# Seven half products for eight: the feed-forward column pairs of a two-layer hybrid network on one core

## Chip, core and metric

The kernel runs on one core of one Trainium2 chip. The metric is device time in microseconds of one execution. The kernel before takes 2122.2 us, the median of three runs (2119.26 to 2122.68).

## What is computed

Two layers over 512 tokens of width 1024, all in fp32. Each layer has a feed-forward block, a mixer (in layer 0 latent attention and a gated delta rule, in layer 1 sparse attention), a second feed-forward block and a gated embedding (PLE). The change touches the four feed-forward blocks:

```python
def swiglu(h, w_gu, w_down):          # w_gu: 1024 x 5632, w_down: 2816 x 1024
    g, u = jnp.split(h @ w_gu, 2, axis=-1)
    return (jax.nn.silu(g) * u) @ w_down

for i in range(DEPTH):
    x = x + 0.5 * swiglu(rms_norm(x, ln_ffn1[i]), ffn1_w_gu[i], ffn1_w_down[i])
    ...                               # x = x + mixer(rms_norm(x, ln_mix[i]))
    x = x + 0.5 * swiglu(rms_norm(x, ln_ffn2[i]), ffn2_w_gu[i], ffn2_w_down[i])
    ...                               # x = x + sigmoid(rms_norm(x, ln_ple[i]) @ w_gate) * (p[i] @ w_in)
```

## The kernel before

The activations lie transposed: x is eight tiles of 128 features by 512 tokens. `prep` multiplies each by its norm gain and splits it into a high part (fp32r) and a low part (the rest); the row factor of the norm, `rB`, is applied to results instead. `mm3` makes one fp32 product from three fp32r matmuls: high by high, high by low, low by high. Each is a 128x128 weight tile against 512 token columns.

`ffn` goes over 22 column pairs j. A pair is column block j of the gate half of `w_gu` and block j of the up half, 128 columns each. For each, `proj` calls `weights`, which loads 1024x128 weights in one DMA of 512 KB on SP into a `raw` tile, casts the high part on ACT and subtracts the low part on DVE (`split`, whose subtraction may also go to POOL as `flex`). It then runs eight k-steps of `mm3` into one PSUM bank. The gate is multiplied by rB (DVE), goes through Silu (ACT) and is multiplied by rB again (POOL); the up result times that is the activation, split again into two big tiles that stay until the down projection. After all 22 pairs the down projection goes over eight output blocks d, each with 22 k-steps in three weight loads; the result is added to x[d] by DVE and `prep(d)` follows for the next stage.

Inside the mixers `weights` splits another way (`split_dma`): ACT writes the high part and minus the weights, and POOL issues a DMA that adds the raw weights to the latter.

The order of instructions on every engine is written out ahead by `Order.issue`. Each operation has a price (`price`, line 335 on); the list scheduler keeps a clock for each engine, takes the ready operation with the smallest key (its place in TensorE's program order, less a part of its longest way to the end), and fixes the order. Tiles come from pools with limits: 58 big tiles of 2 KB a partition (`c`), 4 raw and 3 + 3 split weight tiles of 4 KB, 8 temporaries, 8 PSUM banks. Every tile operation is emitted at one line, L313, so groups in the profile are told apart by tile names: `raw_t`, `wh_t` and `wl_t` are weights, `c_t` big tiles, `t_t` temporaries, `p_t` PSUM banks, `x` the residual.

The start loads x, and the first weights of the first pair between the x tiles (`first`, `early`).

Of the kernel before, what the change touches and what calls it, by code (L numbers as in the profile page):

```python
# [17 lines left out]
P = 128  # L18
# [65 lines left out]
class Op:  # L84
    __slots__ = ("eng", "fn", "cost", "preds", "succs", "tiles", "left", "ready", "done", "forms", "key", "ahead")


KAPPA = 0.9
PEN, TAU, THR = 30.0, 5.0, 0.8
# [3 lines left out]
class Order:  # L93
# [78 lines left out]
    def issue(self):  # L172
# [57 lines left out]
        while len(order) < n:  # L230
# [21 lines left out]
            for e in engines:  # L252
                while idle[e] <= now and avail[e]:
                    i = heapq.heappop(avail[e])[1]
                    tag = fits(i)
                    if tag is not None:
                        blocked[tag].append(i)
                        continue
                    op = ops[i]
                    order.append(i)  # L260
                    issued[i] = True
                    while first < n and issued[first]:
                        first += 1
                    if op.fn[0] == "dma_start":
                        idle[e] = now + (0.45 if e == "sync" else 0.9)
                        dma = max(dma, now + (1.3 if e == "sync" else 2.6)) + op.cost
                        op.done = dma + 0.75
                    else:
                        c = op.cost
                        if e == "tensor":  # L270
                            while edge <= now:
                                cold = worked < (0.85 if cold else 0.45) * self.WINDOW
                                worked, edge = 0.0, edge + self.WINDOW
                            c *= 1 + cold
                            worked += c
                        at = now
                        if shares(op):
                            at = max(now, port)
                            port = at + c
                        idle[e] = op.done = at + c  # L280
                        if e == "vector":
                            recent, since = recent * np.exp((since - now) / TAU) + op.cost / TAU, now
                        if e == "scalar" and op.fn[0] == "activation":
                            new = self.SETS.get(op.fn[1][2], table)
                            if new != table:
                                table, idle[e], op.done = new, idle[e] + 1.28, op.done + 1.28
                    for t in op.tiles:
                        p = pending[t]
                        p.discard(i)
                        if i == last[t]:  # L290
                            tag, lo = self.tag[t], max(p) if p else first - 1
                            if i > lo:
                                use[tag][max(lo + 1, 0):i + 1] -= 1
                            last[t] = lo
                            unblock(tag)
                        if not p:
                            heapq.heappush(ends, (max(ops[u].done for u in users[t]) + 0.2, t))
                    for j in op.succs:
                        s = ops[j]
# [35 lines left out]
def price(eng, method, args, kw, out):  # L335
# [2 lines left out]
    size = lambda x: int(np.prod(x.shape[1:]))  # L338
    n = size(out)
    if method == "dma_start":  # L340
        return n * out.shape[0] * 4 / 335e3
    if eng == "tensor":
        load = size(args[1]) / 1.2e3
        if method == "transpose":
# [16 lines left out]
class Net:  # L361
    def __init__(self, ctx, tc, a):
        self.a, self.mixer = a, False
        pool = lambda name, **k: ctx.enter_context(tc.tile_pool(name=name, **k))
        self.cpool = pool("cpool", bufs=1)
        self.wpool = pool("wpool", bufs=3)
        self.big = pool("big", bufs=58)
# [4 lines left out]
        self.nc, self.early = Order(tc.nc, tc), None  # L372


    def c2(self, dt=F32, shape=(P, S)):
        return self.nc.tile(self.big, 58, shape, dt, "c")

    def t2(self, shape=(P, S)):
        return self.nc.tile(self.tmp, 8, shape, F32, "t")

    def pb(self):
        return self.nc.tile(self.ps, 8, (P, S), F32, "p")
# [14 lines left out]
    def split(self, src, h, l):  # L397

        self.nc.scalar.copy(h, src)
        (self.nc.vector if src.space == PSUM else self.nc.flex).tensor_sub(l, src, raw(h))  # L400

    def split_dma(self, src, h, l):

        nc = self.nc
        nc.scalar.copy(h, src)
        nc.scalar.activation(l, src, AF.Copy, scale=-1.0)
        nc.gpsimd.dma_start(l, src.bitcast(F32R), accum_op=ALU.add)

    def weights(self, *parts):

        parts = [p.rearrange("(k p) c -> p k c", p=P) for p in parts]
        k, n = parts[0].shape[1], sum(p.shape[2] for p in parts)
        w = self.nc.tile(self.wpool, 4, (P, k, n), F32, "raw")
# [4 lines left out]
        h, l = (self.nc.tile(self.wpool, 3, (P, k, n), F32R, t) for t in ("wh", "wl"))  # L418
        (self.split_dma if self.mixer else self.split)(w, h, l)
        return h, l  # L420

    def mm3(self, out, lhs, rhs, start, stop):

        mm = self.nc.tensor.matmul
        mm(out, lhs[0], rhs[0], start=start, stop=False)
        mm(out, lhs[0], rhs[1], start=False, stop=False)
        mm(out, lhs[1], rhs[0], start=False, stop=stop)

    def rsqrt(self, x, name):

# [34 lines left out]
    def prep(self, d, gains, src=None, copy=None):  # L465
# [16 lines left out]
            nc.flex.tensor_add(sq, sq, self.acc)  # L482
        self.acc = sq
        if d == KD - 1:
            self.xn = self.nx
            ms = self.sums(self.acc)
            nc.vector.tensor_scalar(ms, ms, 1.0 / D, EPS, op0=ALU.mult, op1=ALU.add)
            self.r4 = self.rsqrt(ms, "r4")
            pr = self.rows_of(self.r4)
            self.rB = self.small([P, S], "rB")  # L490
            nc.scalar.copy(self.rB, pr)

    def proj(self, *parts):

        w, self.early = self.early or self.weights(*parts), None
# [15 lines left out]
        return ps  # L511


    def start(self, first=None):

        nc, a = self.nc, self.a
        self.idn = self.const([P, P], "idn")
# [19 lines left out]
        load(1)  # L537
        if first is not None:
            early = self.weights(first)
        for d in range(2, KD):  # L540
# [5 lines left out]
        if first is not None:  # L546
            self.early = early

        nc.ahead = 30
        nc.gpsimd.memset(rows2, 0.0)  # L550
# [19 lines left out]
        nc.ahead = 0  # L570


    def ffn(self, w_gu, w_down, nxt):
        nc = self.nc
        act = []
        for j in range(KF):
            pg = self.proj(w_gu[:, j * P:(j + 1) * P])
            pu = self.proj(w_gu[:, DFF + j * P:DFF + (j + 1) * P])
            tg, sg, sr, ab = self.t2(), self.t2(), self.t2(), self.t2()
            nc.vector.tensor_mul(tg, pg, self.rB)  # L580
            nc.scalar.activation(sg, tg, AF.Silu)
            nc.gpsimd.tensor_mul(sr, sg, self.rB)
            nc.vector.tensor_mul(ab, pu, sr)
            h, l = self.c2(F32R), self.c2(F32R)
            self.split(ab, h, l)
            act.append((h, l))
        for d in range(KD):
            py = self.pb()
            for k0, kn in ((0, 8), (8, 8), (16, 6)):
                w = self.weights(w_down[k0 * P:(k0 + kn) * P, d * P:(d + 1) * P])  # L590
                for k in range(kn):
                    self.mm3(py, (w[0][:, k, :], w[1][:, k, :]), act[k0 + k], k0 + k == 0, k0 + k == KF - 1)
            nc.vector.scalar_tensor_tensor(self.x[d], py, 0.5, self.x[d], op0=ALU.mult, op1=ALU.add)
            self.prep(d, nxt)


    def ple(self, p, w_in, w_gate, nxt, out=None):

        nc = self.nc
        pr = self.nc.tile(self.wpool, 4, (P, NT, PLE), F32, "raw")  # L600
        nc.sync.dma_start(pr, p.rearrange("(t p) c -> p t c", p=P))
        pT = []
        for k in range(2):
# [708 lines left out]
```

## Time and profile before

| | |
|---|---|
| profiled execution | 2120.7 us, span 2118.6 us |
| granted TensorE clock, mean | 0.993 |
| feed-forward block 1 | weights loaded from 5 us, down projection from 230, next stage's weights from 352 |
| feed-forward block 2 | 685, 921, 1044 |
| feed-forward block 3 | 1109, 1338, 1460 |
| feed-forward block 4 | 1667, 1903, 2026 |
| even mixer, odd mixer | 352 to 685, 1460 to 1667 |

The stage times are issue times of the first weight loads on SP. PE is TensorE's matmuls, PEld its weight loads, DVE VectorE, ACT ScalarE, POOL GpSimd, SP the queue that issues most DMAs. Busy time of PE is from the start of a matmul to its modelled end, so successive matmuls overlap; distances between starts say how fast they follow each other. A name with q (SPq, POOLq) is the engine's sequencer.

### The profile page before, as it was taken

Reading aid. Unit: us, or ns where it says so; the run is one execution under the profiler, and the core shown is the slowest. Engines: PE = TensorE matmul, PEld = TensorE weight load, DVE = VectorE, ACT = ScalarE, POOL = GpSimd, SP = SyncE. Lnnn points to the kernel's source line nnn. Section 1 sums busy time; section 2 is a strip of 40 time slices with the busy share of each in tenths; the row PEclk is TensorE's granted clock in tenths of the full one; section 3 lists DMA queues with packets and bytes.
Section 4 is the critical chain, followed back from the end, with each engine's and each line's share of the span. In section 5 each row is a group of like instructions: output and inputs, shape, how many; then the busy total and the mean of one; then the engine's idle time right before and its main releaser. Section 6 shows DMA issues by size and latency. Waiting matters only on the chain.

```text
span 2118.6 us, 25037 instructions
## 1 busy us (share of the span) xinstructions
PE 2078.6 (98%) x9586; PEld 1717.9 (81%) x9586; DVE 1047.0 (49%) x2086; ACT 830.2 (39%) x1343; POOL 255.6 (12%) x327
## 2 busy tenths in 40 slices
PE   8999999999989999999999999999999999999998
PEld 6888888878877888888888888888877888888887
DVE  5443333476797533433366433333698544433344
ACT  4333222555485432332233332322668433332232
POOL 1111100133241011110000111100110011110000
PEclk9999999999999999999999999999999999999999
DMA  6333333766331533333233333234672533333332
GB/s 177 95 95 100 94 93 88 169 136 136 95 80 38 132 100 94 96 94 99 88 96 112 99 100 99 87 97 106 146 166 68 119 99 91 99 100 92 92 91 83
DMA packets 374233, 219.36 MB, mean 104 GB/s; under 512 B 17258, under 2 KB 362978, under 8 KB 374114
## 3 DMA queue, kind: packets, MB, share of 16 engines
q1 hardware_dynamic: 365330, 187.30, 30.6%
q0 software_dynamic: 8784, 30.48, 7.6%
q8 instruction: 75, 1.23, 0.2%
q14 instruction: 44, 0.36, 0.1%
HBM read 183.86 MB, written 3.41 MB: 88 GB/s over the span
## 4 chain that ended last, share of the span: by engine, by line
PE 62%; DVE 3%; ACT 1%; issue 0%; ACTq 0%; DVEq 0%
PE p_t L313 62%; DVE c_t L313 2%; DVE m_t L313 1%; ACT t_t L313 1%; ACT c_t L313 1%; DVE t_t L313 0%; ACT wh_t L313 0%; ACT wl_t L313 0%; DVE rs_t L313 0%; DVE rst_t L313 0%; DVE x L313 0%; DVE qss_t L313 0%; DVE rkd_t L313 0%; DVE rqd_t L313 0%; DVE rsh_t L313 0%
## 5 line engine op out<-in xcount | busy, mean ns | idle before, releaser
L313 PE MATMUL p_t<-c_t,wh_t 128*128 128x512 f32 (+1 forms) x5232 | 1600.6, 392 | 5.9 <-ACT wh_t L313 3.9
L313 PEld LDWEIGHTS p_t<-c_t,wh_t 128*128 128x128 f32 (+1 forms) x5232 | 981.0, 188 | 211.6 <-ACT wh_t L313 5.7
L313 PE MATMUL p_t<-c_t,wl_t 128*128 128x512 f32 (+1 forms) x2616 | 993.9, 391 | 0.0
L313 ACT CAST wh_t<-raw_t 128x1024 fp32r<-128x1024 f32 (+2 forms) x365 | 364.0, 998 | 1072.6 <-PE p_t L313 934.0
L313 PEld LDWEIGHTS p_t<-c_t,wl_t 128*128 128x128 f32 (+1 forms) x2616 | 491.6, 188 | 102.6 <-DMA wl_t<-raw_t 0.5
L313 DVE TENSOR_TENSOR wl_t<-raw_t,wh_t 128x1024 fp32r<-128x1024 f32 (+2 forms) x304 | 352.1, 1158 | 215.8 <-ACT wh_t L313 195.2
L313 POOL TENSOR_TENSOR t_t<-t_t,rB_t 128x512 f32<-128x512 f32 x88 | 136.8, 1554 | 1015.8 <-ACT t_t L313 1015.8
L313 DVE TENSOR_TENSOR t_t<-p_t,t_t 128x512 f32<-128x512 f32 x104 | 71.9, 691 | 354.3 <-PE p_t L313 350.1
L313 DVE TENSOR_TENSOR t_t<-p_t,rB_t 128x512 f32<-128x512 f32 x120 | 82.9, 691 | 238.0 <-PE p_t L313 232.1
L313 PE MATMUL p_t<-c_t 128*128 128x128 f32 (+8 forms) x668 | 126.6, 328 | 8.3 <-ACT t_t L313 3.1
L313 PEld LDWEIGHTS p_t<-c_t 128*128 128x128 f32 (+2 forms) x668 | 102.1, 197 | 26.6 <-DVE c_t L313 9.8
L313 POOL DMA_DIRECT2D wl_t<-raw_t x61 | 52.4, 859 | 559.1 <-ACT wl_t L313 537.2
L313 PE MATMUL p_t<-wh_t,c_t 128*128 128x512 f32 (+1 forms) x272 | 83.6, 384 | 0.0
L313 DVE SCALAR_TENSOR_TENSOR x<-p_t,x 128x512 f32<-128x512 f32 x32 | 22.1, 692 | 114.5 <-PE p_t L313 114.5
L313 ACT ACTIVATE t_t<-t_t 128x512 f32<-128x512 f32 x108 | 68.2, 632 | 21.2 <-DVE t_t L313 9.6
L313 ACT ACTIVATE wl_t<-raw_t 128x1024 fp32r<-128x1024 f32 (+4 forms) x61 | 62.1, 1018 | 26.5 <-PE p_t L313 26.2
L313 DVE TENSOR_TENSOR c_t<-p_t,c_t 128x512 fp32r<-128x512 f32 (+5 forms) x116 | 55.3, 518 | 24.6 <-ACT c_t L313 24.2
L313 ACT CAST c_t<-t_t 128x512 fp32r<-128x512 f32 x88 | 54.7, 622 | 20.5 <-DVE t_t L313 18.0
L313 DVE TENSOR_TENSOR c_t<-t_t,c_t 128x512 fp32r<-128x512 f32 x88 | 60.3, 685 | 1.4 <-ACT c_t L313 1.4
L313 PEld LDWEIGHTS p_t<-wh_t,c_t 128*128 128x128 f32 x272 | 50.6, 188 | 8.6
L313 ACT CAST c_t<-p_t 128x128 fp32r<-128x128 f32 (+5 forms) x116 | 45.9, 458 | 23.3 <-PE p_t L313 20.6
L313 PE MATMUL p_t<-wl_t,c_t 128*128 128x512 f32 (+1 forms) x136 | 52.0, 385 | 0.0
(189 smaller groups left out, 1056.3 us busy)
## 6 DMA issues: line engine op xcount, KB each, us to landing
raw_t<-in_ffn_w_gu SPq DMA_DIRECT2D x176, 512.0 KB, 3.7
raw_t<-in_ffn_w_down SPq DMA_DIRECT2D x64, 512.0 KB, 3.4
wl_t<-raw_t POOLq DMA_DIRECT2D x55, 512.0 KB, 5.3
raw_t<-in_ffn_w_down SPq DMA_DIRECT2D x32, 384.0 KB, 3.1
raw_t<-in_even_w_in SPq DMA_DIRECT2D x21, 512.0 KB, 4.0
raw_t<-in_ple_w_gate SPq DMA_DIRECT2D x16, 512.0 KB, 3.6
raw_t<-in_odd_w_in SPq DMA_DIRECT2D x16, 512.0 KB, 4.1
raw_t<-in_even_w_out SPq DMA_DIRECT2D x8, 512.0 KB, 4.0
```

What stands on the lines that cost most here:

```text
L313: self.tc.keep_in_program_order(getattr(getattr(self.nc, op.eng), method)(*args, **kw))
```

## The change

In 20 of the 22 pairs the gate and up columns are computed together. Two neighbouring blocks of k (d and d + 1), the two column blocks (gate and up) and the two halves of the tokens make a product of 2 x 2 blocks, for which eight block products are needed plainly. The new `seven_products` uses seven (Strassen's scheme in Winograd's form): each product has 4 k-steps of `mm3`, with 256 token columns. `seven_weights` makes the seven weight operands from four loads: three blocks are split as they are (`split_dma`, in 512-wide pieces), four are sums and differences made and split by DVE and ACT. `seven` makes four combined and split activation operands of each pair of k-blocks, once a block. The products accumulate in three half banks a, b and c; a and b are read out between products and used on.

Pairs 0 and 1 (`PLAIN`) are computed as before, and `seven` stands after them. The 22 pairs come in runs of 4, 4, 4, 4, 4 and 2, and the down projection of a run is spread between the pairs of the next run: each `down(d, ...)` loads its weights, has a PSUM bank of its own and adds to x[d]. It uses minus one half, because the activation now carries a minus sign. In the feed-forward block DVE does what POOL did (the multiplication by rB and the subtractions of the splits).

Around this: 66 big tiles (58); 7 split weight tiles in one pool (3 + 3); `rB` has one buffer (2); another price for DMAs that POOL issues; no early weights at the start; 1,024 bytes of SBUF a partition for the descriptors of POOL's DMAs instead of the default 16,384.

```diff
+NCT, NW, NRAW = 66, 7, 4
+HALF = S // 2
+PLAIN = 2
+RUNS = (4, 4, 4, 4, 4, 2)
...
-                        dma = max(dma, now + (1.3 if e == "sync" else 2.6)) + op.cost
+                        dma = max(dma, now + (1.3 if e == "sync" else 2.2)) + op.cost
...
-        return n * out.shape[0] * 4 / 335e3
+        return n * out.shape[0] * 4 / (200e3 if "accum_op" in kw else 335e3)
...
+    def split_here(self, src, h, l):
+        self.nc.scalar.copy(h, src)
+        self.nc.vector.tensor_sub(l, src, raw(h))
...
-        (self.split_dma if self.mixer else self.split)(w, h, l)
+        (self.split_dma if self.mixer else self.split_here)(w, h, l)
...
-            self.rB = self.small([P, S], "rB")
+            self.rB = self.small([P, S], "rB", 1)
...
+    def seven(self, d):
+        nc, lo, hi = self.nc, slice(0, HALF), slice(HALF, S)
+        b1, b2, tb = (self.c2() for _ in range(3))
+        for i, b in enumerate((b1, b2)):
+            nc.scalar.activation(b, self.x[d + i], AF.Copy, scale=self.xgains[:, d + i:d + i + 1])
+        nc.vector.tensor_sub(b1[:, lo], b1[:, lo], b1[:, hi])
+        nc.vector.tensor_add(tb[:, hi], b2[:, hi], b1[:, lo])
+        nc.vector.tensor_sub(tb[:, lo], tb[:, hi], b2[:, lo])
+        nc.vector.tensor_sub(b1[:, hi], b2[:, hi], b1[:, hi])
+        (h1, l1), (h2, l2), (ha, la), (hb, lb) = *self.xn[d:d + 2], *([self.c2(F32R) for _ in range(2)] for _ in range(2))
+        self.split_here(b1, ha, la)
+        self.split_here(tb, hb, lb)
...
+    def seven_weights(self, load):
+        nc = self.nc
+        w1, w2, sa, sb = (f(shape=(P, 2, 4, P)) for f in (self.raw4, self.raw4, self.w4, self.w4))
+        load(w1, 0)
+        load(w2, 1)
+        o1, o2, o3, o4, o5, o6, o7 = ([self.c2(F32R, (P, 4, P)) for _ in range(2)] for _ in range(7))
+        for src, (h, l) in ((w1[:, 0], o1), (w1[:, 1], o2), (w2[:, 1], o4)):
+            self.split_dma(src, h, l)
+        nc.vector.tensor_add(sa[:, 0], w2[:, 0], w2[:, 1])
+        self.split_here(sa[:, 0], *o5)
+        nc.vector.scalar_tensor_tensor(sb[:, 0], sa[:, 0], -1.0, w1[:, 0], op0=ALU.mult, op1=ALU.subtract)
+        self.split_here(sb[:, 0], *o6)
+        nc.vector.tensor_sub(sb[:, 1], w1[:, 1], sb[:, 0])
+        self.split_here(sb[:, 1], *o3)
+        nc.vector.tensor_add(sa[:, 1], w1[:, 0], w2[:, 0])
+        self.split_here(sa[:, 1], *o7)
+        return o1, o2, o3, o4, o5, o6, o7
+
+    def seven_products(self, w, x):
+        nc = self.nc
+        a, b, c = (self.pb()[:, :HALF] for _ in range(3))
+        g, v = self.t2(), self.t2()
+        def product(out, i, start):
+            (h, l), n = w[i - 1], len(x)
+            for k in range(n):
+                self.mm3(out, (h[:, k], l[:, k]), x[k][i - 1], start and k == 0, k == n - 1, True)
+        product(a, 1, True)
+        nc.copy(g[:, :HALF], a)
+        product(c, 2, True)
+        product(b, 5, True)
+        nc.copy(v[:, :HALF], b)
+        product(a, 6, False)
+        nc.copy(g[:, HALF:], a)
+        nc.vector.tensor_add(g[:, :HALF], c, g[:, :HALF])
+        product(b, 3, False)
+        product(a, 7, False)
+        nc.copy(v[:, HALF:], a)
+        product(a, 4, False)
+        nc.vector.tensor_add(g[:, HALF:], b, g[:, HALF:])
+        nc.vector.tensor_add(v[:, HALF:], v[:, :HALF], v[:, HALF:])
+        return g, a, v[:, HALF:]
...
+        def column(j):
...
+            g, u1, u2 = self.seven_products(self.seven_weights(load), xs)
+            nc.vector.tensor_mul(g, g, self.rB)
+            nc.scalar.activation(g, g, AF.Silu)
+            ab, h, l = self.t2(), self.c2(F32R), self.c2(F32R)
+            nc.vector.tensor_mul(g, g, self.rB)
+            nc.vector.tensor_mul(ab[:, :HALF], u1, g[:, :HALF])
+            nc.vector.tensor_mul(ab[:, HALF:], u2, g[:, HALF:])
+            nc.scalar.copy(h, ab)
+            nc.vector.tensor_sub(l, ab, raw(h))
+            return h, l
...
+        def down(d, j0, act):
+            py, n = self.pb(), len(act)
+            w, h, l = (self.c2(dt, (P, n, P)) for dt in (F32, F32R, F32R))
+            nc.sync.dma_start(w, w_down[j0 * P:(j0 + n) * P, d * P:(d + 1) * P].rearrange("(k p) c -> p k c", p=P))
+            self.split_here(w, h, l)
+            for k in range(n):
+                self.mm3(py, (h[:, k], l[:, k]), act[k], k == 0, k == n - 1)
+            nc.vector.scalar_tensor_tensor(self.x[d], py, -0.5, self.x[d], op0=ALU.mult, op1=ALU.add)
+            if j0 + n == KF:
+                self.prep(d, nxt)
+
+        before, act, j0 = [], [], 0
+        for n in RUNS:
+            act = []
+            for i in range(n):
+                act.append((plain if j0 + i < PLAIN else column)(j0 + i))
+                if j0 + i == PLAIN - 1:
+                    xs = [self.seven(d) for d in range(0, KD, 2)]
+                for d in range(KD * i // n, KD * (i + 1) // n):
+                    if before:
+                        down(d, j0 - len(before), before)
+            before, j0 = act, j0 + n
+        for d in range(KD):
+            down(d, j0 - len(before), before)
...
-        self.start(a["ffn1_w_gu"][0][:, :P])
+        self.start()
...
-    nc = bacc.Bacc("TRN2", target_bir_lowering=False, num_devices=1)
+    nc = bacc.Bacc("TRN2", target_bir_lowering=False, num_devices=1, dynamic_dma_scratch_size=1024)
```

More of the change, by code (lines that the diff above doesn't have):

```diff
@@ L365, in __init__ @@
         self.cpool = pool("cpool", bufs=1)
-        self.wpool = pool("wpool", bufs=3)
-        self.big = pool("big", bufs=58)
+        self.wpool = pool("wpool", bufs=NW)
+        self.big = pool("big", bufs=NCT)
         self.tmp = pool("tmp", bufs=8)
@@ L371, in __init__, with w4, raw4 @@
         self.dram = pool("dram", bufs=1, space=bass.MemoryType.DRAM)
-        self.nc, self.early = Order(tc.nc, tc), None
+        self.nc = Order(tc.nc, tc)
     def c2(self, dt=F32, shape=(P, S)):
-        return self.nc.tile(self.big, 58, shape, dt, "c")
+        return self.nc.tile(self.big, NCT, shape, dt, "c")
     def t2(self, shape=(P, S)):
         return self.nc.tile(self.tmp, 8, shape, F32, "t")
+    def w4(self, dt=F32, shape=(P, 2, 512)):
+        return self.nc.tile(self.wpool, NW, shape, dt, "w")
+    def raw4(self, shape=(P, 2, 512)):
+        return self.nc.tile(self.wpool, NRAW, shape, F32, "raw")
     def pb(self):
@@ L412, in weights @@
         k, n = parts[0].shape[1], sum(p.shape[2] for p in parts)
-        w = self.nc.tile(self.wpool, 4, (P, k, n), F32, "raw")
+        w, h, l = self.raw4((P, k, n)), self.w4(F32R, (P, k, n)), self.w4(F32R, (P, k, n))
         at = 0
@@ L417, in weights, with mm3 @@
             at += p.shape[2]
-        h, l = (self.nc.tile(self.wpool, 3, (P, k, n), F32R, t) for t in ("wh", "wl"))
-        (self.split_dma if self.mixer else self.split)(w, h, l)
+        (self.split_dma if self.mixer else self.split_here)(w, h, l)
         return h, l
-    def mm3(self, out, lhs, rhs, start, stop):
+    def mm3(self, out, lhs, rhs, start, stop, go_on=False):
         mm = self.nc.tensor.matmul
-        mm(out, lhs[0], rhs[0], start=start, stop=False)
-        mm(out, lhs[0], rhs[1], start=False, stop=False)
-        mm(out, lhs[1], rhs[0], start=False, stop=stop)
+        kw = dict(skip_group_check=True) if go_on else {}
+        mm(out, lhs[0], rhs[0], start=start, stop=False, **kw)
+        mm(out, lhs[0], rhs[1], start=False, stop=False, **kw)
+        mm(out, lhs[1], rhs[0], start=False, stop=stop, **kw)
     def rsqrt(self, x, name):
@@ L489, in prep @@
             pr = self.rows_of(self.r4)
-            self.rB = self.small([P, S], "rB")
+            self.rB = self.small([P, S], "rB", 1)
             nc.scalar.copy(self.rB, pr)
+    def seven(self, d):
[10 more added lines that the diff above has]
+        self.split_here(tb, hb, lb)
+        part = lambda h, l, at: (h[:, at], l[:, at])
+        return (part(h1, l1, lo), part(h2, l2, lo), part(h2, l2, hi), part(hb, lb, lo), part(ha, la, lo), part(hb, lb, hi),
+                part(ha, la, hi))
     def proj(self, *parts):
-        w, self.early = self.early or self.weights(*parts), None
+        w = self.weights(*parts)
         ps = self.pb()
@@ L511, in proj_by_token, with start @@
         return ps
-    def start(self, first=None):
+    def start(self):
         nc, a = self.nc, self.a
@@ L536, in start @@
         nc.vector.tensor_copy(self.G1, pg[:, 0:16])
[L537 to L540, printed above, removed]
+        for d in range(1, KD):
             load(d)
@@ L545, in start @@
             self.prep(d, self.G1, self.turned([xs[d][:, t, :] for t in range(NT)]), self.x[d])
-        if first is not None:
-            self.early = early
         nc.ahead = 30
@@ L573, in ffn @@
     def ffn(self, w_gu, w_down, nxt):
         nc = self.nc
[L575 to L586, printed above, removed]
@@ L587, in ffn @@
-        for d in range(KD):
[L588 to L594, printed above, removed]
+        by = w_gu.rearrange("(i h p) c -> p h i c", h=2, p=P)
@@ new lines, in column, with load @@
+        def column(j):
+            def load(dst, which):
+                for h in range(2):
+                    nc.sync.dma_start(dst[:, h], by[:, h, :, which * DFF + j * P:which * DFF + (j + 1) * P])
+            g, u1, u2 = self.seven_products(self.seven_weights(load), xs)
[8 more added lines that the diff above has]
+            return h, l
@@ new lines, in plain @@
+        def plain(j):
+            ps = []
+            for which in range(2):
+                w = self.weights(w_gu[:, which * DFF + j * P:which * DFF + (j + 1) * P])
+                p = self.pb()
+                for k in range(KD):
+                    self.mm3(p, (w[0][:, k], w[1][:, k]), self.xn[k], k == 0, k == KD - 1)
+                ps.append(p)
+            g, ab, h, l = self.t2(), self.t2(), self.c2(F32R), self.c2(F32R)
+            nc.vector.tensor_mul(g, ps[0], self.rB)
+            nc.scalar.activation(g, g, AF.Silu)
+            nc.vector.scalar_tensor_tensor(g, g, -1.0, self.rB, op0=ALU.mult, op1=ALU.mult)
+            nc.vector.tensor_mul(ab, ps[1], g)
+            self.split_here(ab, h, l)
+            return h, l
@@ L597, in ple @@
     def ple(self, p, w_in, w_gate, nxt, out=None):
         nc = self.nc
-        pr = self.nc.tile(self.wpool, 4, (P, NT, PLE), F32, "raw")
+        pr = self.raw4((P, NT, PLE))
         nc.sync.dma_start(pr, p.rearrange("(t p) c -> p t c", p=P))
```

2 lines of the change are left out of this document (1 added, 1 removed).

## The prediction

> **What bounds the kernel now.** The page comes first: how long the span is and which engine is full.
>
> ```profile
> span 2118.6 us, 25037 instructions
> ...
> PE 2078.6 (98%) x9586; PEld 1717.9 (81%) x9586; DVE 1047.0 (49%) x2086; ACT 830.2 (39%) x1343; POOL 255.6 (12%) x327
> ```
>
> An average of 98% hides what the stages are like, so next come the busy times by stretch (columns: stretch, its length, then the busy time of each engine with its count, granted clock, DMA share, GB/s): the column part and the down part of the first feed-forward block, then the even and the odd mixer.
>
> ```profile
> core 0: us, PE busy (x) PEld busy (x) DVE busy (x) ACT busy (x) POOL busy (x), PEclk, DMA share, GB/s
> 30.00:225.00 195.00, 195.00 (x862) 161.48 (x862) 79.08 (x92) 62.80 (x75) 29.32 (x19) 1.00 0.34 98
> 225.00:350.00 125.00, 125.00 (x553) 103.53 (x553) 43.47 (x49) 34.69 (x42) 4.67 (x3) 1.00 0.32 97
> 350.00:680.00 330.00, 312.64 (x1710) 261.72 (x1708) 234.54 (x770) 195.67 (x399) 88.19 (x200) 0.98 0.46 104
> 1460.00:1665.00 205.00, 197.56 (x940) 158.91 (x939) 150.51 (x463) 129.68 (x324) 19.94 (x24) 0.99 0.50 117
> ```
>
> In the feed-forward block TensorE never stops, at full clock; DVE and ACT are under half busy. The idle time lies in the mixers. The last question is what ends TensorE's waits in a whole block; the wait list of the second block (680 to 1043 us) holds one entry for it, at the block's entry:
>
> ```profile
> engine line waited for: us in total, times, longest us
> PE p_t L313 <- ACT wh_t L313: 3.9, 1, 3.9
> ```
>
> So a feed-forward block costs what its matmuls cost, one after another, and time saved there on TensorE is time saved, as long as the other engines keep up.
>
> **The main term: matmul spacing.** Busy times of matmuls overlap, so I take start-to-start distances from the timeline: first 128x512 in a feed-forward block, then 128x256 with fresh weights for each in the odd mixer, then 128x128 with fresh weights (merged rows: start, length, count).
>
> ```profile
> 203.97 1.07 PE L313 MATMUL p_t<-c_t,wh_t 128*128 128x512 f32 x4
> 204.88 0.62 PE L313 MATMUL p_t<-c_t,wl_t 128*128 128x512 f32 x2
> 205.33 0.61 PE L313 MATMUL p_t<-c_t,wh_t 128*128 128x512 f32 x2
> ```
> ```profile
> 1516.93 0.88 PE L313 MATMUL p_t<-c_t 128*128 128x256 f32 x6
> ...
> 1517.41 0.40 PE L313 MATMUL p_t<-c_t 128*128 128x256 f32 x2
> ...
> 472.71 1.50 PE L313 MATMUL p_t<-c_t,t_t 128*128 128x128 f32 x12
> ```
>
> Six starts lie between 203.97 and 205.33: 0.227 us each. Between 1516.93 and 1517.41 there are four (the second row is the last two of the first row's six): 0.120 us each. Halving the width thus costs 0.0065 us more than half. [...]
>
> A column pair is now 2 projections x 8 k-steps x 3 matmuls = 48 of 512 columns: 48 x 0.227 = 10.90 us. With seven products it is 7 x 4 k-steps x 3 = 84 of 256: 84 x 0.120 = 10.08 us. That is 0.82 us a pair; with the unrounded 0.2267, 0.80. There are 20 pairs x 4 blocks = 80: **64 us less**. [...] The rounding of that row (0.48 us over four steps, 0.118 to 0.122) gives 50 to 77. I take 64.
>
> [...]
>
> **What else the change adds, and what hides it.** Combining the products takes elementwise work. DVE's cost from the timeline, back to back, in one feed-forward column:
>
> ```profile
> 216.48 0.69 DVE L313 TENSOR_TENSOR t_t<-p_t,t_t 128x512 f32<-128x512 f32 x1 [4.06 <-PE p_t L313]
> 217.09 1.23 DVE L313 TENSOR_TENSOR wl_t<-raw_t,wh_t 128x1024 fp32r<-128x1024 f32 x1
> 218.23 0.68 DVE L313 TENSOR_TENSOR c_t<-t_t,c_t 128x512 fp32r<-128x512 f32 x1
> ```
> ```profile
> L313 ACT CAST c_t<-t_t 128x512 fp32r<-128x512 f32 x88 | 54.7, 622 | 20.5 <-DVE t_t L313 18.0
> ...
> L313 DVE TENSOR_TENSOR c_t<-p_t,c_t 128x256 fp32r<-128x256 f32 x8 | 3.3, 415 | 0.0
> ...
> L313 ACT CAST c_t<-p_t 128x256 fp32r<-128x256 f32 x8 | 3.1, 386 | 0.0
> ```
>
> A 512-wide DVE operation holds the engine 0.61 us (216.48 to 217.09), a 256-wide one about 0.34 (its 0.415 less the same 0.08 of overlap). In a seven-product pair DVE does eight 512-wide operations on weights (four low parts, four sums), three on the activation (two scalings, one low part) and five of 256: 11 x 0.61 + 5 x 0.34 = 8.4 us; four 256-wide copies out of PSUM go to DVE or ACT, so DVE has 8.4 to 9.8 us. ACT has ten casts or copies of weights, one Silu and one cast: 12 x 0.62 = 7.5 us, and up to 4 x 0.39 more: at most 9.0. Both are under the pair's 10.08 us of TensorE. The 528 matmuls of the down projection (0.227 each; a group for a run of four is 12 of them, 2.72 us) are spread between pairs, two groups a pair, and add 5.4 us of TensorE against 2 x (0.61 + 0.61) = 2.4 on DVE and 1.2 on ACT. Per pair then: TensorE 15.5, DVE at most 12.2, ACT 10.2. DVE goes from 40% of TensorE's time (79 of 195) to at most 79% and does not reach it. Only the pairs of the first run have no down groups between them; there DVE is at 8.4 to 9.8 of 10.08.
>
> Preparing the four activation combinations (`seven`, per pair of k-blocks four 256-wide and two 512-wide DVE operations, 2.6 us, and four of ACT, about 2.7) is 10.4 us of DVE a block. It lies beside the two plain pairs, 21.8 us of TensorE, in which DVE has 2 x (2 x 1.14 + 4 x 0.61) = 9.4 of its own: cost nothing, unless those weights' own splits come late too; without that cover it would be 10.4 a block.
>
> The weights' low parts come in part through accumulating DMAs, three a pair of 256 KB, issued by POOL:
>
> ```profile
> wl_t<-raw_t POOLq DMA_DIRECT2D x55, 512.0 KB, 5.3
> ...
> wl_t<-raw_t POOLq DMA_DIRECT2D x2, 384.0 KB, 3.8
> ...
> wl_t<-raw_t POOLq DMA_DIRECT2D x2, 192.0 KB, 3.4
> ```
> ```profile
> L313 POOL TENSOR_TENSOR t_t<-t_t,rB_t 128x512 f32<-128x512 f32 x88 | 136.8, 1554 | 1015.8 <-ACT t_t L313 1015.8
> ...
> L313 POOL DMA_DIRECT2D wl_t<-raw_t x61 | 52.4, 859 | 559.1 <-ACT wl_t L313 537.2
> ```
> ```profile
> q1 hardware_dynamic: 365330, 187.30, 30.6%
> q0 software_dynamic: 8784, 30.48, 7.6%
> ```
>
> About 3.5 us from issue to landing, behind 2 x 0.62 of ACT and 0.86 of POOL: 5.6 us from raw weights to both parts. POOL has 2.6 us a pair and loses its 1.55 us multiply. 240 such DMAs of 0.26 MB are 63 MB, at the second queue's 7.6% for 30.5 MB some 16% more DMA time on 38%: no bound. SP issues twice as many weight loads of half the size, the same bytes in the same 512-byte rows. The smaller descriptor store for POOL's DMAs (with two or three of them in flight) and the start, whose first weights no longer go ahead of the last x tiles, are put at nothing, 1 us either way: the first weights were one 512 KB load among 2 MB of x.
>
> **Waits that the change brings.** Products 6, 7 and 4 add to PSUM tiles that are copied out in between. How soon a copy can start shows here: last matmul of a group, then its reader.
>
> ```profile
> 199.21 0.39 PE L313 MATMUL p_t<-c_t,wl_t 128*128 128x512 f32 x1
> ...
> 199.64 0.69 DVE L313 TENSOR_TENSOR t_t<-p_t,rB_t 128x512 f32<-128x512 f32 x1 [2.48 <-PE p_t L313]
> ```
>
> 0.43 after its start, 0.20 after its 0.227 slot; with 0.39 for the copy, TensorE can go on some 0.6 to 0.75 us after product 7 (and as long after 6 and 5, but there another product of 1.44 us lies between). Behind the waiting matmul stands all of TensorE's queue. What fills the place between 7 and 4 is the next pair's first product or a group of the down projection (2.72 us), if the written-out order has put one there. Covered, it is 0; uncovered, 80 x 0.65 = 52 us. I take 0.1 us a pair, **8 us**, nearer to the covered end since the block's TensorE waits now come to a single one in 363 us. At the end of a block stand eight down groups of only two k-steps, 6 x 0.227 = 1.36 us, and each meets 0.61 for x, 0.75 less overlap for the low part and perhaps 0.61 for the square sum, 1.3 to 1.9 of DVE: 1.5 us a block, **6 us** (0 to 18). The mixers are compiled into another order by eight more big tiles and another DMA price; their 25 us of idle can move either way, 6 us each side, taken at 0.
>
> **Sum.** The profiled execution took 2120.7 us, 2.1 more than its span, and the median of the runs is 1.5 above it. 2120.7 - 64 + 8 + 6 = 2070.7, and at the median **2072 us**.
>
> **Rivals.**
> 1. *The order does not cover the PSUM waits.* 0.4 to 0.65 us at most pairs leave 12 to 32 us of the 64: 2090 to 2118. For it: three such points a pair and ACT and DVE with queues where there were none. Against: an 0.65 us hole is small beside a 2.72 us filler. Chance 0.16, of it 0.03 within 0.2%.
> 2. *Weights come late for want of tiles: slower.* All split weights now live in the 66 big tiles. Of these 16 hold x, 16 its combinations, 16 the activations of two runs at a run's end; 18 remain for 14 of a pair's weights and three for each down group. Where the next pair's splits can't begin before the present pair's products free tiles, the 5.6 us chain shows. If half of it does in the last two pairs of each full run, 2.8 x 40 = 112 us: 2122 - 64 + 112 = 2170. It decides from 1.6 us at each of these 40 pairs. Against: pairs of tiles come free every 1.44 us, and down groups (5.4 us a pair) fill. Chance 0.11.
> 3. *The weight load bounds at this width.* The page has it longer than 0.120:
>
> ```profile
> L313 PEld LDWEIGHTS p_t<-c_t,wh_t 128*128 128x128 f32 (+1 forms) x5232 | 981.0, 188 | 211.6 <-ACT wh_t L313 5.7
> ```
>
>    At 0.188 a matmul a pair is 15.8 us and the kernel 2122 + 80 x 4.9 = 2514. Against: the 128x256 and the 128x128 rows, each with fresh weights, at 0.120 and 0.111; loads overlap. Chance 0.02. [...]
> 4. *More than the sum*: waits covered and the mixers' idle shrinks by over 15 us: below 2052. Chance 0.05.
>
> **How the numbers follow.** The forecast keeps 0.66, 2052 to 2090. The range takes in the saving's bounds (50 to 77), both ends of the waits and most of rival 1: 2050 to 2106; outside stay rivals 2 and 3 and the end of 1. About 0.2%, 4 us, is what a measurement of this kernel can tell from no change. Faster by more: 0.66 + 0.13 + 0.05 = 0.84; within: 0.03; slower: 0.13.
>
> **What would show it.** Right: merged rows of 128x256 matmuls at 0.120 apart in the blocks, a block near 343 us plus a few, DVE at 65 to 80% there, TensorE's wait list with many short entries that sum to under 30 us. Rival 1: waits of p_t for ACT or DVE reading p_t, near 0.6 us, by the eighty. Rival 2: waits of p_t for c_t written by ACT, DVE or the accumulating DMA, of 2 us and more, at the ends of runs. I am wrong if 128x256 matmuls in the blocks lie over 0.13 apart, or if TensorE's waits in them sum to over 50 us.

## The result and the profile after

The changed kernel takes **2076.6 us**, the median of four runs (2072.0 to 2078.5), beside 2122.4 for the kernel before: a ratio of 0.978 (95% interval 0.977 to 0.980), some 46 us less. The forecast was 2072 us. The profiled execution took 2075.8 us.

The page of the changed kernel, top line, engine totals, the two main DMA queues, the busiest POOL group (count, then busy time and mean ns of one) and two rows of DMA issues (count, KB each, us to landing):

```profile
span 2074.0 us, 35038 instructions
...
PE 2022.8 (98%) x12466; PEld 1797.3 (87%) x12466; DVE 1661.9 (80%) x3629; ACT 1160.9 (56%) x2133; POOL 373.2 (18%) x506
...
q1 hardware_dynamic: 369426, 187.31, 31.6%
q0 software_dynamic: 43344, 93.41, 26.0%
...
L318 POOL DMA_DIRECT2D c_t<-raw_t x240 | 207.8, 866 | 1040.4 <-ACT c_t L318 825.1
...
raw_t<-in_ffn_w_gu SPq DMA_DIRECT2D x320, 256.0 KB, 3.9
c_t<-raw_t POOLq DMA_DIRECT2D x240, 256.0 KB, 3.8
```

The split weights and the activations now share the name `c_t`, and every line is L318. TensorE issues 2880 matmuls more, and is still busy for 98% of a shorter span. DVE has gone from 49% to 80%. The 240 accumulating DMAs land after 3.8 us (3.5 was assumed), and the second queue moves 63 MB more.

The busy times by stretch of the changed kernel, same columns as before: the middle of the first feed-forward block, the even mixer, the fourth block.

```profile
core 0: us, PE busy (x) PEld busy (x) DVE busy (x) ACT busy (x) POOL busy (x), PEclk, DMA share, GB/s
125.00:315.00 190.00, 190.00 (x1311) 176.89 (x1310) 150.77 (x289) 100.16 (x173) 32.84 (x41) 1.00 0.66 149
362.00:672.00 310.00, 289.07 (x1591) 240.50 (x1590) 248.02 (x792) 184.93 (x373) 97.77 (x163) 0.98 0.45 99
1630.00:1955.00 325.00, 325.00 (x2149) 298.30 (x2148) 267.29 (x506) 179.55 (x298) 52.01 (x60) 1.00 0.63 146
```

In the blocks TensorE is full at full clock, with DVE at 79% (150.8 of 190) and 82%. What ends TensorE's waits there, from 30 to 300 us of the changed kernel, is one entry, which belongs to the norm at the block's entry:

```profile
engine line waited for: us in total, times, longest us
PE p_t L318 <- DVE r_t L318: 1.2, 1, 1.2
```

The pace, from the timeline of the changed kernel inside one product chain (start, length, count):

```profile
150.88 3.04 PE L318 MATMUL p_t<-c_t 128*128 128x256 f32 x24
```

23 steps in 3.04 less one duration of 0.283: 0.120 us each.

**Where the time went.** I add up all start-to-start distances of TensorE's matmuls in the two traces. The *work* is each matmul at its own pace (0.2267 us for 512 columns, 0.1735 for 384, 0.120 for 256, 0.111 for 128); *waits* are what distances hold beyond that, where it is over 12 ns (a lower granted clock counts there too). The work, which follows from these paces and the counts of matmuls, goes from 2038.7 to 1974.6 us, **64.1 less**; the waits from 81.05 to 97.03, **16.0 more**; small differences in pace add 3.4. Together 44.7 less, and the spans differ by 44.6. By stage the waits are (the even mixer from 352 to 685 us before, from 362 to 672 us in the changed kernel):

| | start and first block | even mixer | rest |
|---|---|---|---|
| before | 11.3 | 45.8 | 23.9 |
| changed | 18.5 | 49.6 | 28.9 |

Of the first column's 7.2 us more, 5.5 lie ahead of 50 us. In the rest, blocks 2, 3 and 4 have 2.1, 2.2 and 1.1 us more, and the odd mixer's 19.2 became 18.7. So a quarter of what the matmuls promised was lost: 5.5 us at the start and 3.8 in the even mixer, which the change was not about, and about 7 in the four blocks, some 3 of it inside them and 4 at their ends.

The start, in the wait lists and timelines of the two kernels. Changed, 0 to 40 us:

```profile
PE p_t L318 <- DVE c_t L318: 6.6, 1, 6.6
...
PE p_t L318 <- POOL t_t L318: 2.0, 1, 2.0
...
PE p_t L318 <- DVE r_t L318: 1.2, 1, 1.2
```

Then the first projection, changed and before:

```profile
19.25 5.47 PE L318 MATMUL p_t<-c_t,w_t 128*128 128x512 f32 x17
```
```profile
15.98 1.19 PE L313 MATMUL p_t<-c_t,wh_t 128*128 128x512 f32 x2 [1.07 <-DVE c_t L313]
```

It begins 3.3 us later. Two more waits follow that the kernel before does not have there, for the squares of the norm (`t_t`, 2.0) and for its inverse root (`r_t`, 1.2).

### The profile page after: what moved, and what is told of

Same layout as the page of the kernel before. It is cut to its first block, busy times and chain, and to the rows that moved or that the text cites. A ratio compares the mean times of both kernels' runs of the same rounds, so it can differ in the third digit from the quotient of the medians.

```text
span 2074.0 us, 35038 instructions
## 1 busy us (share of the span) xinstructions
PE 2022.8 (98%) x12466; PEld 1797.3 (87%) x12466; DVE 1661.9 (80%) x3629; ACT 1160.9 (56%) x2133; POOL 373.2 (18%) x506
## 4 chain that ended last, share of the span: by engine, by line
PE 85%; DVE 9%; DMA 2%; ACT 2%; issue 1%; POOL 1%; SPq 0%; ACTq 0%; DVEq 0%; POOLq 0%
PE p_t L318 85%; DVE c_t L318 5%; DVE t_t L318 2%; ACT c_t L318 1%; DVE m_t L318 1%; ACT t_t L318 1%; DMA c_t<-in_ffn_w_down 1%; DMA raw_t<-in_ffn_w_gu 1%; DVE rst_t L318 1%; POOL t_t L318 0%; DMA c_t<-dTt 0%; DVE w_t L318 0%; DMA c_t<-in_x 0%; DMA raw_t<-in_ple_w_gate 0%; ACT w_t L318 0%
## 5 line engine op out<-in xcount | busy, mean ns | idle before, releaser
L318 PE MATMUL p_t<-c_t 128*128 128x256 f32 (+3 forms) x9500 | 1423.7, 310 | 16.1 <-DVE c_t L318 7.9
L318 PEld LDWEIGHTS p_t<-c_t 128*128 128x128 f32 (+1 forms) x9500 | 1301.4, 191 | 130.6 <-DVE c_t L318 16.4
L318 PE MATMUL p_t<-c_t,w_t 128*128 128x512 f32 (+1 forms) x1896 | 460.3, 396 | 0.4 <-DVE w_t L318 0.4
L318 PEld LDWEIGHTS p_t<-c_t,w_t 128*128 128x128 f32 (+1 forms) x1896 | 350.1, 187 | 75.1 <-DVE w_t L318 0.9
L318 POOL DMA_DIRECT2D c_t<-raw_t x240 | 207.8, 866 | 1040.4 <-ACT c_t L318 825.1
L318 ACT CAST c_t<-w_t 128x512 fp32r<-128x512 f32 x320 | 192.8, 619 | 167.6 <-PE p_t L318 152.3
L318 DVE TENSOR_TENSOR c_t<-w_t,c_t 128x512 fp32r<-128x512 f32 x320 | 218.9, 687 | 82.6 <-PE p_t L318 77.1
L318 DVE TENSOR_TENSOR c_t<-c_t 128x512 fp32r<-128x512 f32 (+7 forms) x352 | 185.6, 539 | 44.6 <-PE p_t L318 23.4
L318 ACT CAST c_t<-raw_t 128x512 fp32r<-128x512 f32 x240 | 148.2, 618 | 110.7 <-PE p_t L318 109.4
L318 ACT ACTIVATE c_t<-raw_t 128x512 fp32r<-128x512 f32 x240 | 151.2, 630 | 65.1 <-PE p_t L318 52.7
L318 DVE SCALAR_TENSOR_TENSOR x<-p_t,x 128x512 f32<-128x512 f32 x192 | 130.4, 685 | 57.0 <-PE p_t L318 56.1
L318 ACT CAST c_t<-c_t 128x512 fp32r<-128x512 f32 (+2 forms) x230 | 127.2, 588 | 86.5 <-PE p_t L318 66.4
L318 ACT CAST w_t<-raw_t 128x1024 fp32r<-128x1024 f32 (+5 forms) x109 | 100.4, 935 | 115.5 <-PE p_t L318 101.7
L318 DVE COPY t_t<-p_t 128x256 f32<-128x256 f32 x303 | 127.8, 422 | 19.5 <-PE p_t L318 18.8
L318 DVE TENSOR_TENSOR t_t<-p_t,t_t 128x256 f32<-128x256 f32 (+1 forms) x264 | 116.6, 443 | 24.2 <-PE p_t L318 17.9
L318 ACT CAST c_t<-t_t 128x512 fp32r<-128x512 f32 x88 | 54.7, 622 | 133.7 <-DVE t_t L318 95.8
L318 DVE TENSOR_TENSOR t_t<-t_t,rB_t 128x512 f32<-128x512 f32 x160 | 109.8, 686 | 18.6 <-ACT t_t L318 16.8
L318 DVE TENSOR_TENSOR w_t<-raw_t,w_t 128x512 f32<-128x512 f32 (+2 forms) x128 | 100.1, 785 | 25.9 <-PE p_t L318 22.9
L318 DVE TENSOR_TENSOR w_t<-raw_t 128x512 f32<-128x512 f32 x160 | 109.2, 683 | 6.3 <-DMA raw_t<-in_ffn_w_gu 6.1
L318 POOL DMA_DIRECT2D w_t<-raw_t x61 | 53.1, 876 | 329.6 <-ACT w_t L318 291.1
L318 DVE TENSOR_TENSOR t_t<-t_t 128x256 f32<-128x256 f32 (+1 forms) x196 | 92.0, 469 | 1.8 <-ACT t_t L318 0.6
L318 PE MATMUL p_t<-w_t,c_t 128*128 128x512 f32 (+1 forms) x408 | 93.1, 383 | 0.0
```

What stands on the lines that cost most here:

```text
L318: self.tc.keep_in_program_order(getattr(getattr(self.nc, op.eng), method)(*args, **kw))
```

## The experiments

Times are medians, ratios are to the kernel before on the same chip, and the last three columns are the waits of the profiled execution, worked out as above (start and first block, even mixer, rest). They belong to one execution each: the changed kernel's own columns differ by up to 2 us between its two profiles, and the profiled execution with three copies, 2081.2 us, lies 4.9 above its median.

| | us | ratio (95%) | start | even | rest |
|---|---|---|---|---|---|
| changed, again | 2074.8 | 0.979 (0.978 to 0.981) | 16.4 | 51.4 | 27.7 |
| all pairs plain | 2171.7 | 1.023 (1.022 to 1.025) | 16.8 | 86.7 | 26.4 |
| all plain, down weights in the weight pools | 2138.0 | 1.008 (1.007 to 1.009) | 17.2 | 52.0 | 30.4 |
| 12 plain pairs a block | 2150.5 | 1.013 (1.012 to 1.015) | 20.9 | 90.2 | 27.7 |
| blocks 3 and 4 all plain | 2106.7 | 0.994 (0.992 to 0.995) | 21.1 | 50.2 | 24.8 |
| three copies more in the hole | 2076.3 | 0.978 (0.977 to 0.980) | 29.2 | 47.2 | 26.9 |
| no accumulating DMAs | 2074.9 | 0.978 (0.977 to 0.979) | 20.1 | 49.2 | 26.6 |
| 58 big tiles | 2087.9 | 0.983 (0.981 to 0.985) | 21.0 | 43.3 | 37.1 |
| no plain pairs | 2086.8 | 0.983 (0.980 to 0.985) | 33.5 | 44.8 | 38.5 |
| old DMA price | 2080.4 | 0.980 (0.979 to 0.982) | 19.8 | 51.8 | 26.3 |
| early weights | 2068.7 | 0.975 (0.974 to 0.977) | 18.4 | 41.1 | 28.8 |
| early weights, `seven` later in the order | 2067.4 | 0.975 (0.974 to 0.976) | 17.8 | 42.1 | 29.3 |

**Is the gain the seven products?** The first try kept the new order of runs and made all pairs plainly:

```diff
-PLAIN = 2
+PLAIN = 22
-                if j0 + i == PLAIN - 1:
+                if j0 + i == PLAIN - 1 < KF - 1:
```

> All 22 pairs plain, with the runs, the spread down projection, the pools and prices of the changed kernel; no seven-product pair is left. Theory (TensorE's matmul spacing sets the time): 80 pairs give back 0.80 us each, 64 us, and the 520 places where a 512-wide matmul is followed by a 256-wide one, 0.0065 us each, vanish (3.4): 2076.6 + 64 - 3 = 2137, from 2130 to 2144, slower than before. Rival (the spread down projection and the bigger pools bring part of the gain): 2122 or less.

It took 2171.7 us, 35 more than that. The work was the 2038.7 of the kernel before, but the even mixer's waits had doubled. The stretch of this kernel that holds the even mixer:

```profile
375.00:715.00 340.00, 298.91 (x1525) 248.00 (x1524) 239.54 (x765) 177.31 (x347) 86.53 (x151) 0.90 0.45 105
```

The granted clock is 0.90 there, 0.98 in the changed kernel. SP's timeline of this kernel shows what stands between the mixer's loads:

```profile
396.66 0.37 SPq L318 DMA_DIRECT2D raw_t<-in_even_w_in  x1
397.12 0.54 SPq L318 DMA_DIRECT2D c_t<-in_ffn_w_down  x1
...
522.07 0.39 SPq L318 DMA_DIRECT2D c_t<-in_ffn_w_down  x1
...
590.29 0.37 SPq L318 DMA_DIRECT2D c_t<-in_ffn_w_down  x1
```

These are down weights of the second block, loaded 300 us ahead into big tiles, which the plain pairs no longer need and the mixer does. Of that block's 48 such loads 31 are issued before its first gate and up weights (739 us), 23 of them from 397 us on. The changed kernel loads ahead too, but fewer: ten at the end of the first block, and the next at 797 us.

```profile
353.52 7.83 SPq L318 DMA_DIRECT2D c_t<-in_ffn_w_down  x10
```

So a new theory: the excess is this hoarding. Its test takes the down weights from the weight pools instead:

```diff
-            w, h, l = (self.c2(dt, (P, n, P)) for dt in (F32, F32R, F32R))
+            w, h, l = self.raw4((P, n, P)), self.w4(F32R, (P, n, P)), self.w4(F32R, (P, n, P))
```

> All 22 pairs plain as in e1, but the down projection's weights come from the raw and split weight pools in place of three big tiles each. Theory (e1's 34 us over its expectation are the second block's down weights, loaded into big tiles some 300 us early, during the even mixer, which then lacks tiles): the even mixer's TensorE waits fall from about 85 us to 40 to 55, its granted clock rises from 0.90 to 0.97 or more, and the kernel takes the 2137 first expected of e1, from 2125 to 2144. Rival (the mixer's written-out order is bad for another reason): 2160 to 2180.

It took 2138.0 us, and the same stretch of it reads:

```profile
371.00:690.00 319.00, 294.53 (x1620) 248.96 (x1619) 241.52 (x776) 198.16 (x408) 94.03 (x167) 0.96 0.51 113
```

34 us went, nearly all in the even mixer (86.7 to 52.0), and no down weights are loaded ahead any more. Whether the early loads hurt through the tiles that they hold or through the transfers was not separated. This kernel is also the control: all of the change but the seven products, apart from the down weights' pools. It costs 17 us more than the kernel before on that chip (2120.8), and the seven products then bring 2138.0 - 2074.8 = 63 us, where 64 was the term of the sum. In the traces the two spans differ by 65: 64.1 of work and 4.1 of waits, less 2.9 of pace. Half of the seven products should bring half. The next kernel makes pairs of blocks 3 and 4 plainly:

```diff
+        self.nffn = getattr(self, "nffn", 0) + 1
+        first = PLAIN if self.nffn <= 2 else KF
-                act.append((plain if j0 + i < PLAIN else column)(j0 + i))
-                if j0 + i == PLAIN - 1:
+                act.append((plain if j0 + i < first else column)(j0 + i))
+                if j0 + i == first - 1 < KF - 1:
```

> Blocks 1 and 2 as changed, all 22 pairs of blocks 3 and 4 plain: 40 seven-product pairs in place of 80, and the even mixer between unchanged neighbours. Theory (matmul spacing): 2076.6 + 40 x 0.80 - 1.7 = 2107, from 2101 to 2113, the even mixer's waits as in the changed kernel. Rival (the gain of a pair is not the same in every block, or the plain form costs elsewhere): under 2098 or over 2120.

2106.7 us, with its runs between 2101.5 and 2113.8: 31.9 above the changed kernel on that chip, half of 64. An earlier try at a half, with `PLAIN = 12` in every block, did not say this; its combined activations are made from an x to which the first down groups have already been added, so it computes something else, and only its time is read.

> Twelve of 22 pairs plain instead of two, so 40 seven-product pairs instead of 80. Theory: half of the gain, 2076.6 + 40 x 0.80 - 1.7 = 2107, from 2100 to 2113, and no TensorE wait in the blocks. Rival (DVE limits the denser stretches, so the last pairs gain less than the first): less than half is lost, under 2098.

It took 2150.5 us. Its even mixer has the doubled waits too (90.2), and SP issues the early down loads in it between 393 and 702 us; without those 40 us it would lie near 2110.

**Do the PSUM waits stand open (rival 1)?** Three more copies were put into the hole between products 7 and 4, where TensorE would stand if nothing filled it:

```diff
+        for _ in range(3):
+            nc.scalar.copy(v[:, HALF:], a)
```

> Between products 7 and 4 the PSUM tile a is copied out four times in place of once, three times by ACT: the wait that product 4 must sit out grows from about 0.65 to 1.4 us. Theory (other matmuls fill that place): 0 to 8 us more, 2075 to 2084, no waits of TensorE for ACT or DVE in the blocks. Rival 1 of the prediction (the place is not filled): 80 x 0.79 = 63 more, about 2140.

2076.3 us, no difference, and from 675 to 1005 us the wait list of TensorE is empty. The order fills the hole with more than 1.2 us of other matmuls. The timeline shows how: of the down projection's 2112 matmuls, 512 wide, in the changed kernel 373 stand alone between 256-wide ones, not in groups of 12.

**Does DVE have room, and do the accumulating DMAs matter?** One word changes in `seven_weights`:

```diff
-            self.split_dma(src, h, l)
+            self.split_here(src, h, l)
```

> The three plain weight blocks of a pair are split by ACT and DVE instead of ACT and an accumulating DMA: DVE has 3 x 0.61 = 1.8 us more a pair, ACT 1.9 less, POOL issues no DMA in the blocks. Theory (DVE has room: at most 12.2 + 1.8 = 14.0 of 15.5 us a pair): 0 to 10 us more, lost in the first runs alone, where DVE has 10.2 to 11.6 of 10.08: 2077 to 2087. Rival (DVE is as good as full): 80 x 1.8, over 2150.

2074.9 us, the same. The fourth block of this kernel:

```profile
1630.00:1950.00 320.00, 320.00 (x2124) 295.07 (x2123) 284.82 (x531) 154.78 (x262) 4.13 (x4) 1.00 0.36 100
```

DVE does three more subtractions a pair and is at 89% (284.8 of 320 us), ACT does three operations less, and TensorE's wait lists of the blocks hold 0.4 us beside the norm at the first entry. So neither the 63 MB of added DMA traffic nor the load on DVE cost anything at this point, and the accumulating DMAs bring nothing.

**Are the big tiles short (rival 2)?** Their number was put back from 66 to 58:

```diff
-NCT, NW, NRAW = 66, 7, 4
+NCT, NW, NRAW = 58, 7, 4
```

> The changed kernel with 58 big tiles in place of 66: at a run's end 10 are left for 14 of a pair's weights and three for a down group. Theory (matmul spacing sets the time, tiles are not short at 66): waits appear in the blocks now, of 0.3 to 1 us a pair, 2095 to 2150, since 10 is under what one pair holds. Rival (tiles come free so fast that eight make no difference): under 2082. If tiles were short already at 66, over 2150.

2087.9 us, between the two theories. The chain that rival 2 feared now shows in the wait list, 30 to 330 us of this kernel:

```profile
PE p_t L318 <- DMA c_t<-raw_t: 2.0, 4, 1.4
```

Over the four blocks it is near 7 us. With 66 tiles there is no such entry. Even with 8 fewer, they are far from the 112 us of rival 2. The profiled execution was 2079.7 us; what the other 8 us of the median are, its trace cannot show; the three longer executions had a granted clock of 0.988 to 0.989, this one 0.994.

**What do the two plain pairs hide?** Without them `seven` stands ahead of the first pair:

```diff
-PLAIN = 2
+PLAIN = 0
+        xs = [self.seven(d) for d in range(0, KD, 2)]
```

> No plain pair: the combined activations are prepared ahead of pair 0. Theory of the prediction (preparing them costs 10.4 us of DVE a block, hidden by the two plain pairs alone): 8 more pairs save 6.4, and 4 x 10.4 come onto the path: 2076.6 - 6.4 + 41.6 = 2112, from 2098 to 2118. Rival (the end of the stage before and the first products, which need no combination, hide it as well): 2070 to 2080.

2086.8 us, about 11 above the changed kernel, though 8 pairs more save 6.4: some 17 us of `seven` and late weights lie open, of the 41.6 us that it was priced at. The waits moved where they should: the first block's entry has 26.9 us up to 50 us (16.7 in the changed kernel) and block 3's entry 9.2 (1100 to 1150 us; 0.9), while at the entries of blocks 2 and 4 none appears. The ends of the first and third block have 6.2 and 5.9 (1.3 and 1.0), but a first block's end of 2.7 to 3.3 is also found in kernels with the two plain pairs (no accumulating DMAs, old DMA price). Theory and rival each missed: the cover is worth less than all of `seven`, because at two of the four entries nothing lies open without it.

**Where do the losses at the start and in the even mixer come from?** First, the price by which the order of the DMAs is planned was put back:

```diff
-                        dma = max(dma, now + (1.3 if e == "sync" else 2.2)) + op.cost
+                        dma = max(dma, now + (1.3 if e == "sync" else 2.6)) + op.cost
-        return n * out.shape[0] * 4 / (200e3 if "accum_op" in kw else 335e3)
+        return n * out.shape[0] * 4 / 335e3
```

> The changed kernel with the order's old price for DMAs that POOL issues (2.6 us and 335 GB/s in place of 2.2 and 200). Theory (the even mixer's 6 us of additional waits come from the new price): its waits fall from 50 to about 44 and the kernel takes 2070. Rival (the written-out order of the mixer shifts with anything ahead of it): waits anywhere from 40 to 90, the blocks without waits all the same, 2066 to 2116.

2080.4 us, and the even mixer has 51.8 us of waits. The price is not it; this theory fell. Then the first weights were loaded between the x tiles again, as before the change:

```diff
-        for d in range(1, KD):
+        load(1)
+        early = self.weights(first)
+        for d in range(2, KD):
             load(d)
...
+        self.early = early
...
-        self.start()
+        self.start(a["ffn1_w_gu"][0][:, :P])
```

> The changed kernel with the first weights loaded and split between the x tiles again, as before the change. Theory (the start lost 7 us of TensorE waits because the first weights' low part now stands on DVE behind all of x): the waits up to 40 us go from 18.5 back to about 11, the kernel takes 2076 - 7 = 2069, from 2064 to 2073, if the mixers' order stays. Rival (the start is set by x alone, as the prediction had it): the same waits and 2075 to 2078.

2068.7 us, the time that was expected, for a reason that was not. The first projection does begin at 16.0 us again, but TensorE then stands for the inverse root. Timeline of this kernel, TensorE and then DVE (some rows):

```profile
38.01 1.09 PE L318 MATMUL p_t<-idn,r_t 128*128 128x128 f32 x4 [5.16 <-DVE r_t L318]
```
```profile
30.30 0.15 DVE L318 TENSOR_TENSOR rst_t<-rst_t,rsh_t 128x4 f32<-128x4 f32 x1
35.87 0.69 DVE L318 TENSOR_TENSOR w_t<-raw_t 128x512 f32<-128x512 f32 x1 [5.42 <-DMA raw_t<-in_ffn_w_gu]
36.48 0.15 DVE L318 SCALAR_TENSOR_TENSOR r_t<-rst_t,r_t 128x4 f32<-128x4 f32 x1
```

The root's small steps are done one at a time in DVE's order; between two of them stands the first sum of `seven_weights`, and it waits 5.4 us for its weights. SP's timeline of this kernel points to why those are late:

```profile
21.79 4.64 SPq L318 DMA_DIRECT2D c_t<-in_ffn_w_down  x5
26.48 7.84 SPq L318 DMA_DIRECT2D raw_t<-in_ffn_w_gu  x7
```

Down weights, not used before the second run of pairs, are loaded ahead of the gate and up weights that are next, while the DMA engines are full (share 1.03 from 33 to 38 us). The start's waits stay at 18.4 us. The gain of 8 us is the even mixer's (49.6 to 41.1). The last kernel tried to take `seven` out of the root's way by a later place in the order, on top of the early weights:

```diff
+                    nc.ahead = 4
                     xs = [self.seven(d) for d in range(0, KD, 2)]
+                    nc.ahead = 0
```

> As e4 (first weights between the x tiles), and the combined activations get a key 4 us later, so that their DVE operations do not stand between the thirteen small ones of the norm's root at the start. Theory (in e4 TensorE waited 5.2 us for that root because a 0.42 us operation of seven stood before each of its steps): that wait falls under 2 us, all waits up to 40 us from 16.6 to about 12, the kernel 2069 - 4 = 2065, from 2061 to 2068. Rival (the root is late for another reason): the wait stays and 2067 to 2072.

2067.4 us lies in the range of the theory and in that of the rival. The wait decides for the rival: the list (0 to 45 us) still has the entry.

```profile
PE p_t L318 <- DVE r_t L318: 5.3, 1, 5.3
```

DVE's timeline has the same 5.5 us wait for `in_ffn_w_gu` between two steps of the root. No gain over the early weights alone is shown (0.975 both); the two are the best versions found, 0.4% below the changed one. Down weights kept from going ahead at the start were not tried with the seven products. The changed kernel once more, beside these:

> The changed kernel itself, on the chip of e9 to e11 for comparison: 2076.6, from 2073 to 2080.

2074.8 us, ratio 0.979 where it was 0.978.

## Why the prediction was right, point by point

- **Matmul spacing, 64 less (50 to 77).** Right: 0.120 us in the blocks, from which the 64.1 us of work follow; as times, 63 by the control and 32 for half of it. The bounds are the rounding of the 128x256 row, 0.118 to 0.122.
- **Elementwise work hidden.** Right. DVE came to 79 and 82% where 65 to 80 was forecast, and even 89% cost nothing. `seven` beside the two plain pairs: hidden, but the price without that cover (41.6 us for four blocks) was too high; 17 were seen.
- **Accumulating DMAs: no bound.** Right; 3.8 us to land, 26.0% of the second queue, and nothing gained or lost without them. The smaller descriptor store was not tried by itself.
- **The start at nothing, 1 us either way.** This step failed: 5.5 us up to 50 us. The all-plain kernels have as much in this column (16.8 and 17.2), so it is not the seven products that cost it. The sum looked at one 512 KB load among 2 MB of x, and not at what is late next. With that load put back, the next wait (5.2 us, the root behind weights that come late, after down weights) took its place. The down weights' 256 KB loads were on the list of the change, and their place in SP's queue was not asked for.
- **PSUM waits, 8 us, and block ends, 6 us.** That the order covers the holes was seen rightly, the sizes were too large: some 3 us more than before inside the four blocks, and at their ends 4.3 in the first profile and 2.4 in the second. At the ends the wait lists mostly name ACT (`t_t`, up to 1.1 us), where DVE was priced. The order interleaves single down matmuls, which the forecast took as groups of 12.
- **The mixers, 0 (6 either way).** Within its bounds for the changed kernel (3.8 in the even one, 5.6 in the second profile), but the bounds were too narrow for the thing: over the kernels above the even mixer's waits lie between 41 and 52 us, and near 90 with hoarded tiles.
- **Sum.** 14 us of losses were taken, all of them in the blocks, where 7 came. Another 12 came in terms put at nothing: the start (5.5), the two mixers (3.3) and pace (3.4). The two errors nearly cancel, so that 2072 lies as near to 2076.6 as it does is in part luck.
- **Rivals.** 1 (open PSUM waits) falls by the three copies; 2 (tiles) by the wait list, and shows in a small way at 58 tiles; 3 (weight load) by the 0.120 at 0.187 to 0.191 us of weight load a matmul. The 0.111 that the prediction sets against it is read from its 128x128 row: 1.50 us less one duration of 0.28, over eleven steps. 4 did not come: the even mixer's idle grew. The upper end of rival 1's own range, 2118, does not follow from its sum: 12 us left of 64 give 2110.
- **A reading of the profile before.** The 3.9 us wait that stands in the prediction at the entry of block 2 belongs to the even mixer. In the timeline of the kernel before, the matmul that waited starts while SP has not yet issued the mixer's last output weights, let alone the block's first:

```profile
681.34 1.22 PE L313 MATMUL p_t<-c_t,wh_t 128*128 128x512 f32 x2 [3.93 <-ACT wh_t L313]
```
```profile
682.39 0.37 SPq L313 DMA_DIRECT2D raw_t<-in_even_w_out  x1
685.46 13.32 SPq L313 DMA_DIRECT2D raw_t<-in_ffn_w_gu  x3
```

  Block 2 itself then has no entry in the list at all, which makes the argument built on it stronger.

What stays open: why the even mixer comes out 4 us worse in the changed kernel than before, and 8 better than that with the early weights. Between these last two its instructions are the same and only the order written out differs; both load ten down weights ahead. The DMA price is not the reason.

## What to carry to other kernels

Where the trace shows TensorE full for a whole stage, price a change of shape by the start-to-start distance of that very shape in the same trace; here the control gave 63 us for a forecast of 64. Then look outside the stage: tiles that the change frees or takes, and loads that may now be issued earlier, go to whoever comes first in the written-out order; in the first all-plain kernel this cost 34 us in a mixer that nobody had touched. Before crediting an edit with a gain, look whether the wait it was made for has gone; in two kernels here the time was in the expected range and TensorE still waited as long at the start.

## What the runs showed of the hardware

- In the changed kernel a 512-wide matmul directly behind a 256-wide one takes 235 ns to the next start (mean of 515 places in the blocks), 227 in a row of its kind. That is some 4 us; a 256-wide one behind a 512-wide one takes 117 instead of 120, which gives 1.3 back. Together they are most of the 3.4 us of pace.
- In the early-weights kernel the granted clock was 0.84 around the 5.2 us wait (33 to 38 us) and 0.78 in the 12 us after it, 1.00 in the changed kernel over the same 38 to 50 us. By the clock alone that is an estimate of some 2.6 us more (12 x 0.22). In the kernel with `seven` later in the order, whose wait there was 5.3 us, the clock was 0.80 from 38 to 50 us. Whether the 0.90 of the first all-plain kernel's even mixer (375 to 715 us) comes from its waits in this way, no run separates.
